# Fixing the place of the weight-scale sums and maxima in their engines' queues

## The chip, the cores and the metric

The kernel runs on one NeuronCore of a Trainium2 chip. The metric is the device time of one execution in microseconds; of the kernel before, three runs took 1717.04 to 1720.6 us, with a median of 1719.97 us.

## The reference

One layer of a streaming encoder is applied to 320 frames: 256 of a prompt and 64 of a sample, which share all weights. Cut to its weight products:

```python
xn = rmsnorm(x, norm_mix)
q, k, v, u, vs, g = split(xn @ w_in)           # 2048 -> 9216 columns
a  = stick_breaking_attention(q, k, v)         # prompt: causal; sample: with a cache of 256
bb = spatial_gate(gelu(u), rmsnorm(gelu(vs)))
merged = sigmoid(g_a) * (a @ w_branch_a) + sigmoid(g_b) * (bb @ w_branch_b)
h  = x + merged @ w_out
gu = rmsnorm(h, norm_ffn) @ w_gate_up          # 2048 -> 2 x 5632
h  = h + (silu(gu[..., :5632]) * gu[..., 5632:]) @ w_down
y  = rmsnorm(h, norm_final)
```

All of it is float32. The kernel has to return y, the new k and v rows and the sample's normalised v rows.

## The kernel before, in words

Features lie on the 128 partitions and the 320 frames along the free axis. Every weight matrix is read once, in **weight tiles** of 128 x 1024 float32 (512 KB, eight blocks of 128 x 128). A tile is loaded by a transfer that SP issues, split into a high part wh (ACT) and a low part wl (DVE), and used by PE in 24 products of 128 x 128 by 128 x 320: for each block wh with the activation's high part, wh with its low part, wl with its high part (lines 90, 91 and 92, in `product`). wh and wl have four buffers each, so ACT and DVE can be four tiles ahead of PE. The program counts tiles: `tick()` is called after the products of each, and `at(tick, fn)` runs a piece of code at that count.

The change concerns the **FFN**. Its 44 column groups are taken in three slices of 16, 16 and 12. A slice has a gate/up stage, then a down stage with w_down (float32 parts, wraw's three buffers; 32 tiles in slices one and two). A group is four tiles: two for the gate column block and two for the up column block. Below, tile (g,i) is tile i of group g.

Groups 0 to 2 run as float32 parts (`weights`, lines 82 and 83). From group 3 (`PLAIN`) on the products are in float16 (`block16`): wh is the weight times a power of two, rounded to float16 (ACT, line 785), wl the remainder (DVE, line 786), and the activations X are float16 pairs, made from h in `normed` (lines 747 on DVE, 749 on ACT, 750 on DVE). The power of two has to be known before the first wh of the group. It comes from a **scale** per group (`class Scale`):

- each raw tile gives one number per partition: the sum of magnitudes on ACT (`sum`, line 174) or the largest magnitude on DVE (`top`, line 170). From group 5 on tiles 0 and 2 get sums and tiles 1 and 3 maxima; groups 3 and 4 have four sums.
- `pack` (lines 180 and 182, DVE: topmost, packed) makes one number per partition of the four; `spread` (line 186, PE: one small product) lays it across all partitions; `close` (lines 190 to 192 and 777, DVE: peak, down, up, undo) makes the factors of it.

Raw tiles of these groups have a pool of their own, raw16, with 14 buffers. A load into it (line 759, issued by SP) must wait until the tile that had the buffer was read by its sum or maximum, its wh and its wl. The program text asks for these steps at fixed counts before the group's first product: the load of tile i at 11 − i tiles before it, the sum or maximum at 8 − i, the spread at 4, the closing at 3:

```python
at(max(start_of(j) - 11 + i, base + 1), group_load, j, i)
at(start_of(j) - 8 + i, group_top, j, i)
at(start_of(j) - 4, lambda j=j: groups[j]["scale"].spread())
at(start_of(j) - 3, group_close, j)
```

That is the order in which instructions are *traced*, not the order in which they stand in the queues. Each engine executes its queue strictly in order, and a scheduler fills the queues: it may put an instruction whose inputs it takes to be ready ahead of others that were traced before it. `tc.keep_in_program_order(ins)` takes this freedom away for one instruction: it stays behind the instruction that was traced last before it on its engine. Before the change the spread is fixed in this manner, sums and maxima are not. After the two blocks of a group, ACT takes the results out of PSUM (`finish16`, lines 821 and 822, ev with Silu and bb), DVE multiplies them (line 823) and the product is split into two parts A (line 128 on ACT, line 129 on DVE) for w_down.

Of the kernel before, what the change touches and what calls it, by code (L numbers as in the profile page):

```python
# [13 lines left out]
AF = mybir.ActivationFunctionType  # L14
ALU = mybir.AluOpType
# [25 lines left out]
def stream_step(ctx: ExitStack, tc: tile.TileContext, xT, w_in, w_a, w_b, w_out, w_gu, w_down,  # L41
                gains, ws_t, bs, ck_t, cv, y_t, k_t, v_t, sv_t):
    nc = tc.nc
# [119 lines left out]
    class Scale:  # L163
# [3 lines left out]
            self.tops = const.tile([P, n], F32, tag=f"tops{n}", bufs=2, name="tops")  # L167

        def top(self, i, src):
            nc.vector.tensor_reduce(out=self.tops[:, i : i + 1], in_=src, axis=mybir.AxisListType.X, op=ALU.max,  # L170
                                    apply_absolute_value=True)

        def sum(self, i, src, junk):
            nc.scalar.activation(out=junk, in_=src, func=AF.Abs, accum_out=self.tops[:, i : i + 1])  # L174

        def pack(self):
            own = self.tops
# [10 lines left out]
        def close(self):  # L188
            top, self.down, self.up = (const.tile([P, 1], F32, tag=t, bufs=3, name=t) for t in ("peak", "down", "up"))
            nc.vector.tensor_reduce(out=top, in_=self.row[:, :P], axis=mybir.AxisListType.X, op=ALU.max)  # L190
            nc.vector.tensor_tensor(out=self.down.bitcast(I32), in0=top.bitcast(I32), in1=bits, op=ALU.bitwise_and)
            nc.vector.tensor_tensor(out=self.up.bitcast(I32), in0=self.down.bitcast(I32), in1=bits, op=ALU.bitwise_xor)
            return self
# [782 lines left out]
```

## Time and profile before

| | before |
|---|---|
| median of three runs | 1719.97 us (1717.04 to 1720.6) |
| the profiled execution | 1719.68 us |
| its span, first to last instruction | 1717.9 us |
| PE busy | 1665.5 us, 97% |
| DVE busy | 979.6 us, 57% |
| ACT busy | 793.3 us, 46% |
| mean granted clock of PE | 0.996 |

The profile is one execution. Its page gives busy times, the span in 40 slices, DMA queues, the chain of work that ended last, and groups of instructions by line; further views give waits, a timeline and busy times by stretch. A row of the timeline is: start in us from the span's start, length in us, engine, line, operation, result and operands with their sizes, and how often; in brackets the idle time of the engine before it and what ended it. Raw buffers are called raw there whichever pool they are from. PE's products overlap in their pipeline: one is shown 0.30 us long, but the next starts 0.136 us later in the f16 stages.

### The profile page before, as it was taken

The numbers are of one execution on the slowest core, as the hardware profiler recorded it, in microseconds if no ns is written. First come the engines' busy times: TensorE is split into PE (matmuls) and PEld (weight loads), VectorE is DVE, ScalarE is ACT, GpSimd is POOL, SyncE is SP. The second block draws the span as 40 slices with busy tenths as digits, with TensorE's granted clock in tenths as the row PEclk, the third lists the DMA queues.
The fourth block names the chain that finished last, engine by engine and source line by source line (L and its number), as shares of the span: only waits on it lengthen the run. The fifth ranks groups of instructions, "written<-read, shape, count | busy, mean of one in ns | idle before, by whom it ended". The sixth has DMA issues, their size and how long they took to land.

```text
span 1717.9 us, 28001 instructions
## 1 busy us (share of the span) xinstructions
PE 1665.5 (97%) x11586; PEld 1493.7 (87%) x11586; DVE 979.6 (57%) x1430; ACT 793.3 (46%) x1117; POOL 56.9 (3%) x80
## 2 busy tenths in 40 slices
PE   9999999999999999999989899999988999999997
PEld 9999999999999999999656689976666899766797
DVE  6777656544444445559555554456556544556454
ACT  6655545433333334447545532354554423555442
POOL 1200021000000001110000000000000000000000
PEclk9999999999999999999999999999999999999999
DMA  7676656544444445567444455444444554443153
GB/s 256 182 218 169 172 169 169 155 149 147 150 152 152 149 155 169 174 207 256 144 135 143 140 171 149 147 145 138 139 144 136 170 149 141 144 139 99 55 149 122
DMA packets 100512, 268.33 MB, mean 156 GB/s; under 512 B 28993, under 2 KB 35393, under 8 KB 100385
## 3 DMA queue, kind: packets, MB, share of 16 engines
q1 hardware_dynamic: 97936, 261.36, 48.6%
q0 software_dynamic: 1312, 3.80, 0.7%
q8 instruction: 90, 1.47, 0.3%
q10 hardware_dynamic: 1136, 1.39, 0.2%
q14 instruction: 38, 0.30, 0.1%
HBM read 256.03 MB, written 5.51 MB: 152 GB/s over the span
## 4 chain that ended last, share of the span: by engine, by line
PE 68%; DMA 15%; ACT 7%; DVE 6%; issue 3%; ACTq 0%; DVEq 0%
PE acc L92 21%; PE acc L91 21%; PE acc L90 21%; DMA raw<-w_gu 15%; DVE wl L786 5%; ACT wh L785 4%; ACT junk L174 2%; PE aux L289 1%; ACT A L128 1%; PE acc L289 1%; DMA raw<-w_in 1%; PE aux L535 1%; DVE h L900 0%; DVE wl L83 0%; ACT wh L82 0%
## 5 line engine op out<-in xcount | busy, mean ns | idle before, releaser
L90 PE MATMUL acc<-A,wh 128*128 128x320 f32 x1856 | 574.9, 310 | 2.1 <-ACT wh L82 1.7
L92 PE MATMUL acc<-A,wl 128*128 128x320 f32 x1856 | 573.7, 309 | 1.4 <-DVE wl L83 1.4
L91 PE MATMUL acc<-A,wh 128*128 128x320 f32 x1856 | 573.7, 309 | 0.2
L82 ACT CAST wh<-raw 128x1024 fp32r<-128x1024 f32 (+1 forms) x304 | 311.5, 1026 | 521.6 <-PE acc L91 430.2
L83 DVE TENSOR_TENSOR wl<-raw,wh 128x1024 fp32r<-128x1024 f32 (+1 forms) x304 | 363.9, 1198 | 265.2 <-ACT wh L82 264.6
L92 PE MATMUL acc<-X,wl 128*128 128x320 f16 x1312 | 394.4, 301 | 32.8 <-DVE wl L786 32.7
L90 PE MATMUL acc<-X,wh 128*128 128x320 f16 x1312 | 393.9, 300 | 4.0 <-ACT wh L785 3.9
L91 PE MATMUL acc<-X,wh 128*128 128x320 f16 x1312 | 393.7, 300 | 0.0
L90 PEld LDWEIGHTS acc<-A,wh 128*128 128x128 f32 x1856 | 348.5, 188 | 3.3 <-ACT wh L82 2.3
L92 PEld LDWEIGHTS acc<-A,wl 128*128 128x128 f32 x1856 | 348.4, 188 | 1.9 <-DVE wl L83 1.9
L91 PEld LDWEIGHTS acc<-A,wh 128*128 128x128 f32 x1856 | 348.5, 188 | 0.7 <-DVE A L129 0.7
L786 DVE SCALAR_TENSOR_TENSOR wl<-raw,up,wh 128x1024 f16<-128x1024 f32 x164 | 209.8, 1280 | 176.3 <-ACT wh L785 173.8
L92 PEld LDWEIGHTS <-wl 128*128 128x128 f16 x1312 | 128.6, 98 | 99.4 <-DVE wl L786 49.3
L174 ACT ACTIVATE junk<-raw 128x1024 f16<-128x1024 f32 x86 | 90.9, 1056 | 264.5 <-DMA raw<-w_gu 264.4
L785 ACT ACTIVATE wh<-raw,up 128x1024 f16<-128x1024 f32 x164 | 180.3, 1137 | 29.9 <-PE acc L91 29.7
L90 PEld LDWEIGHTS <-wh 128*128 128x128 f16 x1312 | 128.8, 98 | 54.5 <-ACT wh L785 6.7
L91 PEld LDWEIGHTS <-wh 128*128 128x128 f16 x1312 | 128.8, 98 | 48.9
L170 DVE TENSOR_REDUCE tops<-raw 128x1 f32<-128x1024 f32 x78 | 94.6, 1213 | 3.1 <-DMA raw<-w_gu 3.0
L90 PE MATMUL acc<-mh,wh 128*128 128x320 f32 x256 | 79.2, 309 | 0.0
L90 PE MATMUL acc<-B,wh 128*128 128x320 f32 x256 | 79.1, 309 | 0.0
L91 PE MATMUL acc<-B,wh 128*128 128x320 f32 x256 | 79.1, 309 | 0.0
L92 PE MATMUL acc<-B,wl 128*128 128x320 f32 x256 | 79.1, 309 | 0.0
(206 smaller groups left out, 1299.4 us busy)
## 6 DMA issues: line engine op xcount, KB each, us to landing
raw<-w_gu SPq DMA_DIRECT2D x176, 512.0 KB, 3.7
raw<-w_in SPq DMA_DIRECT2D x141, 512.0 KB, 3.8
raw<-w_down SPq DMA_DIRECT2D x80, 512.0 KB, 3.6
raw<-w_out SPq DMA_DIRECT2D x32, 512.0 KB, 3.7
raw<-w_a SPq DMA_DIRECT2D x16, 512.0 KB, 3.6
raw<-w_b SPq DMA_DIRECT2D x16, 512.0 KB, 3.5
raw<-w_down SPq DMA_DIRECT2D x16, 256.0 KB, 2.7
x<-xT SPq DMA_DIRECT2D x8, 320.0 KB, 7.9
```

Source lines behind the costliest of these rows:

```text
L82: nc.scalar.copy(out=wh[:, : n * P], in_=raw[:, : n * P])
L83: nc.vector.tensor_tensor(out=wl[:, : n * P], in0=raw[:, : n * P], in1=wh[:, : n * P].bitcast(F32), op=ALU.subtract)
L90: nc.tensor.matmul(ps[:, :T], a, x[0], start=first, stop=False, skip_group_check=True)
L91: nc.tensor.matmul(ps[:, :T], a, x[1], start=False, stop=False, skip_group_check=True)
L92: nc.tensor.matmul(ps[:, :T], b, x[0], start=False, stop=last, skip_group_check=True)
L128: nc.scalar.copy(out=hi, in_=src)
L170: nc.vector.tensor_reduce(out=self.tops[:, i : i + 1], in_=src, axis=mybir.AxisListType.X, op=ALU.max, apply_absolute_value=True)
L174: nc.scalar.activation(out=junk, in_=src, func=AF.Abs, accum_out=self.tops[:, i : i + 1])
L289: nc.tensor.matmul(first[b][h][:, :T], w[:, (h * n + j) * P : (h * n + j + 1) * P], xs[c + j][i], start=not last and c + j + i == 0, stop= ...
L535: mm = lambda out, a, b, first, last: nc.tensor.matmul(out, a, b, start=first, stop=last, skip_group_check=True)
L785: nc.scalar.activation(out=wh, in_=raw, func=AF.Copy, scale=up)
L786: nc.vector.scalar_tensor_tensor(out=wl, in0=raw, scalar=up, in1=wh, op0=ALU.mult, op1=ALU.subtract)
```

## The change

Both operations on raw tiles are handed to `keep_in_program_order`, so that each stays behind what was traced just before it on DVE or on ACT. Nothing else is edited. Lines after the first edit move by one: what was line 174 is 175, line 785 is 786, and so on.

```diff
         def top(self, i, src):
-            nc.vector.tensor_reduce(out=self.tops[:, i : i + 1], in_=src, axis=mybir.AxisListType.X, op=ALU.max,
-                                    apply_absolute_value=True)
+            tc.keep_in_program_order(nc.vector.tensor_reduce(
+                out=self.tops[:, i : i + 1], in_=src, axis=mybir.AxisListType.X, op=ALU.max, apply_absolute_value=True))
 
         def sum(self, i, src, junk):
-            nc.scalar.activation(out=junk, in_=src, func=AF.Abs, accum_out=self.tops[:, i : i + 1])
+            tc.keep_in_program_order(
+                nc.scalar.activation(out=junk, in_=src, func=AF.Abs, accum_out=self.tops[:, i : i + 1]))
```

The queues of PE, POOL and SP hold the same instructions in the same order as before; those of ACT and DVE differ in the FFN alone, but for the maximum over the norm's gains, which moves on DVE from the start of the program to the w_out stage. Three places follow. In the names, a number marks a tile: (5,0) to (5,3) are raw_8362, raw_8406, raw_8445 and raw_8482, (6,0) is raw_8532, (7,0) to (7,3) are raw_8684, raw_8716, raw_8752 and raw_8787, (8,0) to (8,3) are raw_8836, raw_8868, raw_8904 and raw_8939, (9,0) is raw_8988.

The first is ACT in the middle of the first f16 stage, where the weights of group 5 are made. Before:

```order
L174 ACTIVATE junk,tops<-raw_8836 128x1024
L785 ACTIVATE wh_8799<-raw_8362,up 128x1024
L785 ACTIVATE wh_8838<-raw_8406,up 128x1024
L821 ACTIVATE ev<-acc,undo 128x320
L174 ACTIVATE junk,tops<-raw_8904 128x1024
L785 ACTIVATE wh_8871<-raw_8445,up 128x1024
L785 ACTIVATE wh_8906<-raw_8482,up 128x1024
L822 ACTIVATE bb<-acc,undo 128x320
L174 ACTIVATE junk,tops<-raw_8988 128x1024
```

and with the change:

```order
L175 ACTIVATE junk,tops<-raw_8684 128x1024
L128 CAST A<-bb 128x320
L786 ACTIVATE wh_8799<-raw_8362,up 128x1024
L786 ACTIVATE wh_8838<-raw_8406,up 128x1024
L822 ACTIVATE ev<-acc,undo 128x320
L175 ACTIVATE junk,tops<-raw_8752 128x1024
L786 ACTIVATE wh_8871<-raw_8445,up 128x1024
L786 ACTIVATE wh_8906<-raw_8482,up 128x1024
L823 ACTIVATE bb<-acc,undo 128x320
L175 ACTIVATE junk,tops<-raw_8836 128x1024
```

Beside the same wh there now stand the sums of tiles four loads older: (7,0), (7,2) and (8,0) in place of (8,0), (8,2) and (9,0).

The second is DVE at the same place. Before:

```order
L786 SCALAR_TENSOR_TENSOR wl_8800<-raw_8362,up,wh_8799 128x1024
L170 TENSOR_REDUCE tops<-raw_8868 128x1
L786 SCALAR_TENSOR_TENSOR wl_8839<-raw_8406,up,wh_8838 128x1024
L786 SCALAR_TENSOR_TENSOR wl_8872<-raw_8445,up,wh_8871 128x1024
L170 TENSOR_REDUCE tops<-raw_8939 128x1
L190 TENSOR_REDUCE peak<-aux 128x1
L180 TENSOR_REDUCE topmost<-tops 128x1
L191 TENSOR_TENSOR down<-peak,bits 128x1
L182 TENSOR_SCALAR packed<-topmost 128x1
```

and with the change:

```order
L787 SCALAR_TENSOR_TENSOR wl_8800<-raw_8362,up,wh_8799 128x1024
L787 SCALAR_TENSOR_TENSOR wl_8839<-raw_8406,up,wh_8838 128x1024
L787 SCALAR_TENSOR_TENSOR wl_8872<-raw_8445,up,wh_8871 128x1024
L170 TENSOR_REDUCE tops<-raw_8787 128x1
L191 TENSOR_REDUCE peak<-aux 128x1
L192 TENSOR_TENSOR down<-peak,bits 128x1
L193 TENSOR_TENSOR up<-down,bits 128x1
L778 TENSOR_SCALAR undo<-down,undo_7066 128x1
L170 TENSOR_REDUCE tops<-raw_8716 128x1
L824 TENSOR_TENSOR bb<-bb,ev 128x320
L181 TENSOR_REDUCE topmost<-tops 128x1
```

The maxima are those of group 7 in place of group 8, and that of (7,1) stands behind peak to undo, the closing of group 6: it was traced right after it. Behind topmost follow wl of (5,3), A's low half, packed of group 7 and then wl of (6,0).

The third is ACT at the start of the FFN, from the copies of the norm's factor on; the sums there are those of groups 3 and 4 (raw_7979, raw_8016, raw_8059 and raw_8104 are (3,0) to (3,3)). Before:

```order
L174 ACTIVATE junk,tops<-raw_7979 128x1024
L174 ACTIVATE junk,tops<-raw_8016 128x1024
L82 CAST wh<-raw 128x1024
L220 COPY root<-root 32x10 x3
L174 ACTIVATE junk,tops<-raw_8059 128x1024
L174 ACTIVATE junk,tops<-raw_8104 128x1024
L749 ACTIVATE X<-ev,gain_7064 128x320 x2
L174 ACTIVATE junk,tops<-raw_8159 128x1024
L749 ACTIVATE X<-ev,gain_7064 128x320 x2
```

and with the change:

```order
L221 COPY root<-root 32x10 x3
L750 ACTIVATE X<-ev,gain_7064 128x320 x4
L175 ACTIVATE junk,tops<-raw_7979 128x1024
L82 CAST wh<-raw 128x1024
L814 ACT_TABLE_LOAD
L814 ACTIVATE ev<-ev 128x320
L750 ACTIVATE X<-ev,gain_7064 128x320
L82 CAST wh<-raw 128x1024
L750 ACTIVATE X<-ev,gain_7064 128x320
L175 ACTIVATE junk,tops<-raw_8016 128x1024
L750 ACTIVATE X<-ev,gain_7064 128x320
L82 CAST wh<-raw 128x1024
```

The four sums of group 3 stood around the copies of root; now the first comes behind the first four X, and one follows in each round of X, sum, X and wh. Between two such rounds PE needs one plain tile. In the down stages the sums of the next slice's first groups, which stood at the end of the f16 stage before, now come between the last eight tiles of w_down.

## The prediction

> **What bounds the kernel now.** I read the page's engine and group tables first, then the table of waits, then the timeline of PE, ACT and DVE inside the stretches where PE is not full. PE is busy for 97% of the span, so a gain can only come from its holes. The group table says where they lie: a group's last two numbers are the engine's idle time ahead of it and what ended it.
>
> ```profile
> PE 1665.5 (97%) x11586; PEld 1493.7 (87%) x11586; DVE 979.6 (57%) x1430; ACT 793.3 (46%) x1117; POOL 56.9 (3%) x80
> ...
> L92 PE MATMUL acc<-X,wl 128*128 128x320 f16 x1312 | 394.4, 301 | 32.8 <-DVE wl L786 32.7
> ...
> L174 ACT ACTIVATE junk<-raw 128x1024 f16<-128x1024 f32 x86 | 90.9, 1056 | 264.5 <-DMA raw<-w_gu 264.4
> ...
> raw<-w_gu SPq DMA_DIRECT2D x176, 512.0 KB, 3.7
> ```
>
> PE's holes sit in the f16 gate/up products and end with wl from DVE. ACT, 46% busy, stands 264 us ahead of the sums (L174) waiting for a load. The table of waits adds who holds the loads back:
>
> ```profile
> ACT junk L174 <- DMA raw<-w_gu: 264.4, 77, 5.2
> ...
> SPq L759 <- DVE wl L786: 492.7, 149, 6.1
> ```
>
> A load into raw16 waits until wl has read the tile 14 loads earlier. The timeline of DVE, ACT and PE (start, length, what) shows these two waits closing into a ring:
>
> ```profile
> 873.08 1.28 DVE L786 SCALAR_TENSOR_TENSOR wl<-raw,up,wh 128x1024 f16<-128x1024 f32 x1 [0.56 <-ACT wh L785]
> ...
> 880.29 1.29 DVE L786 SCALAR_TENSOR_TENSOR wl<-raw,up,wh 128x1024 f16<-128x1024 f32 x1 [2.95 <-ACT wh L785]
> 881.50 1.22 DVE L170 TENSOR_REDUCE tops<-raw 128x1 f32<-128x1024 f32 x1
> 882.63 0.28 DVE L190 TENSOR_REDUCE peak<-aux 128x1 f32<-128x128 f32 x1
> ...
> 883.21 0.21 DVE L777 TENSOR_SCALAR undo<-down,undo 128x1 f32<-128x1 f32 x1
> ...
> 884.53 0.49 DVE L823 TENSOR_TENSOR bb<-bb,ev 128x320 f32<-128x320 f32 x1
> ```
>
> ```profile
> 878.07 1.06 ACT L174 ACTIVATE junk<-raw 128x1024 f16<-128x1024 f32 x1 [3.58 <-DMA raw<-w_gu]
> ...
> 879.13 2.17 ACT L785 ACTIVATE wh<-raw,up 128x1024 f16<-128x1024 f32 x2
> 881.21 0.51 ACT L822 ACTIVATE bb<-acc,undo 128x320 f32<-128x320 f32 x1
> ...
> 885.16 1.06 ACT L174 ACTIVATE junk<-raw 128x1024 f16<-128x1024 f32 x1 [3.44 <-DMA raw<-w_gu]
> ...
> 886.21 0.44 ACT L128 CAST A<-bb 128x320 fp32r<-128x320 f32 x1
> ```
>
> ```profile
> 874.42 0.31 PE L92 MATMUL acc<-X,wl 128*128 128x320 f16 x1 [0.88 <-DVE wl L786]
> 881.64 0.31 PE L92 MATMUL acc<-X,wl 128*128 128x320 f16 x1 [0.52 <-DVE wl L786]
> 889.08 0.31 PE L92 MATMUL acc<-X,wl 128*128 128x320 f16 x1 [0.69 <-DVE wl L786]
> ```
>
> The wl that starts at 873.08 ends at 874.36; 3.71 us later, the landing time of a load, the sum at 878.07 starts; wh stands right behind that sum in ACT's queue, wl at 880.29 waits for wh, and its end at 881.57 releases the next load, whose sum starts at 885.16. Once around is 3.7 + 1.06 + 1.1 + 1.28 = 7.1 us, plus 0.44 where the cast to A lies between, and it feeds two weight tiles. PE's stalls come 7.22 and 7.44 us apart. **Latency in a ring, not any engine's work, sets the pace there.**
>
> What two tiles cost without the ring is in the trace too, at the start of the second and third f16 stage, where no stall occurs:
>
> ```profile
> 803.21 0.23 PE L186 MATMUL aux<-turner,packed 128*128 128x128 bf16 x1
> ...
> 994.51 0.30 PE L92 MATMUL acc<-X,wl 128*128 128x320 f16 x1
> ...
> 1110.15 0.23 PE L186 MATMUL aux<-turner,packed 128*128 128x128 bf16 x1
> ...
> 1341.25 0.30 PE L92 MATMUL acc<-X,wl 128*128 128x320 f16 x1
> ...
> 1457.27 0.23 PE L186 MATMUL aux<-turner,packed 128*128 128x128 bf16 x1
> ...
> 1470.38 0.22 PE L186 MATMUL aux<-turner,packed 128*128 128x128 bf16 x1
> ...
> 1621.67 0.30 PE L92 MATMUL acc<-X,wl 128*128 128x320 f16 x1
> ```
>
> From spread to spread, 1457.27 to 1470.38, a group of four tiles takes 13.11 us, so a tile 3.27.
>
> **What can be taken back.** The f16 stages hold 13, 16 and 12 groups. First stage: 803.21 to 994.65 (the last product plus one pitch of 0.14) is 191.4 us, against 13 × 13.11 = 170.4: 21.0 lost. Second: 231.2 against 209.8: 21.4. Third: 164.5 against 157.3: 7.2. Together **49.6 us**. The two down stages between them lose a little as well. There one tile takes 3.52 us, the step from one wh to the next, which wait for PE:
>
> ```profile
> 1043.19 1.05 ACT L82 CAST wh<-raw 128x1024 fp32r<-128x1024 f32 x1 [2.47 <-PE acc L91]
> ...
> 1046.71 1.05 ACT L82 CAST wh<-raw 128x1024 fp32r<-128x1024 f32 x1 [2.47 <-PE acc L91]
> ```
>
> 32 tiles are 112.6 us; from 994.65 to 1110.15 it took 115.5 and from 1341.39 to 1457.27 it took 115.9, so 2.9 + 3.3 = **6.2 us**, lost at their heads, where wh and wl come late out of the same ring. All of it: 55.8 us.
>
> **The change, part by part.** No instruction is added or removed on any engine, and the queues of PE, SP and POOL are the same. ACT's 86 sums and DVE's 78 maxima stand one group, four tiles, later. Take PE working on group 4 from time 0: it is through its tiles at 3.3, 6.5, 9.8 and 13.1, and starts group 5 at 13.1. With the durations above (L821 like L822, L129 like L823, each small step 0.2 like undo) and ACT in the new order:
>
> - wh of (5,0) can start when PE frees the buffer of (4,0), at 3.3, and ends 4.4; (5,1) 6.5 to 7.7; gate's eviction L821 to 8.2; sum (7,2) to 9.4; wh (5,2) 9.8 to 10.9; (5,3) 13.1 to 14.2; L822 to 14.8; sum (8,0) to 16.0; cast to A to 16.4; wh (6,0) to 17.6.
> - DVE: wl (5,2) to 12.2; max (7,3) to 13.4; peak, down, up, undo, which need the spread that PE runs at 13.1, to 14.2; max (7,1) to 15.4; L823 to 15.9; topmost to 16.1; wl (5,3) to 17.3; A's low half to 17.8; packed (7) to 18.0; wl (6,0) to 19.3; then (6,1) at 22.1 and (6,2) at 25.3, which is 12.2 + 13.1: the round closes in PE's own time.
>
> PE needs wl (6,0) at 26.5, it is there 7 us sooner; the tightest of the four, (5,3), has 5.8. packed (7) is asked for at 26.2: 8 us in hand. The sum's load is no longer in the round: tile (7,2) goes into the buffer of (4,0), whose wl ended 13.1 us before that of (5,0), thus at 19.3 − 26.2 = −6.9; plus 3.7 it lands at −3.2 and is summed at 8.2, **11 us of slack** where ACT now waits 3.5. So the stalls of the steady part go entirely, and I credit 49.6 + 6.2.
>
> What moves the other way is the start of the FFN. Before, eight sums slip in ahead; now the four of group 3 come between the plain tiles, and packed (3) may come after PE asks for it:
>
> ```profile
> 760.84 0.31 PE L90 MATMUL acc<-A,wh 128*128 128x320 f32 x1
> ...
> 768.59 1.98 POOL L215 TENSOR_TENSOR root<-ms,mhalf 32x10 f32<-32x10 f32 x1 [11.70 <-DVE ms L213]
> ...
> 770.96 0.62 ACT L220 COPY root<-root 32x10 f32<-32x10 f32 x3
> ...
> 775.87 1.02 ACT L749 ACTIVATE X<-ev,gain 128x320 f16<-128x320 f32 x2
> ...
> 778.89 1.28 ACT L813 ACT_TABLE_LOAD   x1
> ```
>
> PE asks after eight tiles, at 760.84 + 8 × 3.52 = 789.0. ACT's copies of root cannot come sooner than POOL's 770.57. Three sums between them and the fourth X go, but X also waits for ev from DVE, so I let that X end only 0.5 before the 776.9 of now, at 776.4. Then to the last sum of group 3: four sums (4.2), four wh (4.2), the table load (1.3), a Silu (0.5, like L822) and six X (3.1), 13.3 in all: 789.7, and topmost and packed 0.7 later, 790.4. **A single stall of 1.4 us**; bounds are 0, should X end 1.4 us sooner still, and 4, should each later X wait half a microsecond for ev. Behind it group 3's tiles run with one to two us in hand, then the round above is reached. At the later stages the same step has room: the sums of the next groups come from the 25th down tile on, PE asks at the 28th, and ACT is four tiles ahead.
>
> [...] While the ring runs, the clock falls twice (window, engine busy times, then granted clock):
>
> ```profile
> 890.00:900.00 10.00, 8.05 (x52) 4.99 (x50) 4.72 (x11) 3.64 (x5) 0.00 (x0) 0.90 0.42 129
> 900.00:910.00 10.00, 10.00 (x71) 7.01 (x70) 5.57 (x6) 4.67 (x7) 0.00 (x0) 0.93 0.50 159
> 1110.00:1170.00 60.00, 60.00 (x447) 43.26 (x446) 35.98 (x56) 31.69 (x44) 0.00 (x0) 1.00 0.42 141
> 1320.00:1330.00 10.00, 9.65 (x59) 6.46 (x60) 7.78 (x14) 4.42 (x8) 0.00 (x0) 0.83 0.40 133
> ```
>
> Clocks of 0.90, 0.93 and 0.83 over 10 us each are 1.0, 0.7 and 1.7 us of PE. I count these 3.4 us among the stalls, since the full 60 us carry 1.00. [...]
>
> **The sum.** The profiled execution took 1719.68 us, 0.3 below the median of the three runs. 1719.7 − 55.8 + 1.4 = **1665.3 us**.
>
> **Rivals.**
> *Half stays* (chance 0.10). The order closes a new, shorter ring, by DVE's peak: it waits for PE's spread, and a max, wl (5,3) and wl (6,0) are queued behind it. For: DVE now stands there at PE's pace. Against: it is reached at 13.4, after the spread, and 5.8 us remain. If every second stall comes back: 1665.3 + 28 = 1693 us.
> *No change* (0.03). The load itself, not its place in ACT's queue, is the limit, and wh waits where the sum did. For: SP waits 492.7 us for wl. Against: the first product of a tile lies 14 tiles, 45 us, behind the wl that frees its buffer. 1720 us.
> *Slower* (0.05). The sums are too late for the scale: PE reaches the spread before packed and stops, with all products behind it. That costs 41 times the lateness and decides once packed is more than 8 + 1.4 us later than in my round (55.8 / 41 = 1.4 to break even). For: the first group, where I find it late already. Against: 8 us in every other group. Stops of 3 us at each spread would give 1665.3 + 41 × 3 = 1789 us.
>
> **How the numbers follow.** All stalls gone: 0.82, its own range 1660 to 1673 (a first stall of 0 to 4 us, 3.4 for the clock, a few us where the stages meet, 0.2% between runs). That is already 8 in 10 of all cases; I reach up to 1680 for a part of the first rival. 0.2%, 3.4 us, is about what a measurement of this kernel tells from no change: faster 0.92, same 0.03, slower 0.05.
>
> **What would show it.** Right: ACT's idle time ahead of the sums for a load falls from 264 us to under 20; PE's for wl (L92, X) from 32.7 to under 3; spreads 13.1 us apart all through the stages; one stall near 789. Wrong: spreads 13.5 or more apart, or the clock dips with no stall near them. What would make it wrong at one stroke is a load that lands much later than 3.7 us.

## The result, and the profile after

The change makes the kernel faster: **1662.97 us** (median, 1662.5 to 1663.12) against 1719.16 us for the kernel before, run beside it on the same chip (1717.04 to 1720.6). The ratio is 0.9674, with a 95% interval of 0.9657 to 0.969. The forecast was 1665.3, in a range of 1659 to 1680. The profiled execution took 1663.03 us, with a span of 1660.9.

The page of the kernel after, in the order of the page before: the engines, the chain of work that ended last (its shares by engine), the groups, the loads. Line numbers from 174 on are one higher than before.

```profile
PE 1649.9 (99%) x11586; PEld 1498.3 (90%) x11586; DVE 979.8 (59%) x1430; ACT 804.3 (48%) x1117; POOL 56.6 (3%) x80
...
PE 97%; DMA 1%; DVE 1%; ACT 0%; SPq 0%; issue 0%; DVEq 0%; ACTq 0%
...
L92 PE MATMUL acc<-X,wl 128*128 128x320 f16 x1312 | 392.7, 299 | 0.0
...
L786 ACT ACTIVATE wh<-raw,up 128x1024 f16<-128x1024 f32 x164 | 188.1, 1148 | 217.4 <-PE acc L91 213.7
...
L175 ACT ACTIVATE junk<-raw 128x1024 f16<-128x1024 f32 x86 | 89.9, 1045 | 0.0
...
raw<-w_gu SPq DMA_DIRECT2D x176, 512.0 KB, 4.1
```

PE's idle time for wl is gone (32.7 us before, 0.0 now), and so is ACT's 264 us ahead of the sums. ACT now stands 213.7 us ahead of wh, and what ends that wait is PE freeing a buffer. Before, ACT was late for PE; now PE is late for ACT, as it should be when PE is the bound. The chain of work that ended last is PE's to 97% now; in the profile before, its shares were:

```profile
PE 68%; DMA 15%; ACT 7%; DVE 6%; issue 3%; ACTq 0%; DVEq 0%
```

A load takes slightly longer to land (4.1 us where it was 3.7), and no sum or maximum waits for it.

ACT in the middle of the first f16 stage, from the timeline of the kernel after:

```profile
881.21 1.15 ACT L786 ACTIVATE wh<-raw,up 128x1024 f16<-128x1024 f32 x1 [2.11 <-PE acc L91]
...
882.67 1.04 ACT L175 ACTIVATE junk<-raw 128x1024 f16<-128x1024 f32 x1
...
887.78 1.15 ACT L786 ACTIVATE wh<-raw,up 128x1024 f16<-128x1024 f32 x1 [2.11 <-PE acc L91]
...
889.25 1.04 ACT L175 ACTIVATE junk<-raw 128x1024 f16<-128x1024 f32 x1
```

No sum has a wait in brackets; the two wh shown wait 2.1 us for PE, and those between them 0.25 and 0.66. Two tiles take 6.57 us (881.21 to 887.78), where the ring took 7.22 and 7.44.

PE's timeline gives the account by stage, since the same products stand at its borders as before:

```profile
759.88 0.31 PE L90 MATMUL acc<-A,wh 128*128 128x320 f32 x1
...
788.35 0.23 PE L187 MATMUL aux<-turner,packed 128*128 128x128 bf16 x1 [0.15 <-DVE packed L183]
...
802.56 0.23 PE L187 MATMUL aux<-turner,packed 128*128 128x128 bf16 x1
...
907.33 0.22 PE L187 MATMUL aux<-turner,packed 128*128 128x128 bf16 x1
920.43 0.22 PE L187 MATMUL aux<-turner,packed 128*128 128x128 bf16 x1
...
972.62 0.30 PE L92 MATMUL acc<-X,wl 128*128 128x320 f16 x1
...
1085.53 0.23 PE L187 MATMUL aux<-turner,packed 128*128 128x128 bf16 x1
...
1294.88 0.30 PE L92 MATMUL acc<-X,wl 128*128 128x320 f16 x1
...
1407.79 0.23 PE L187 MATMUL aux<-turner,packed 128*128 128x128 bf16 x1
...
1564.75 0.30 PE L92 MATMUL acc<-X,wl 128*128 128x320 f16 x1
```

With 0.14 us added to each last product, as in the prediction:

| stretch | before, us | after, us | gain | predicted |
|---|---|---|---|---|
| up to the FFN's first product | 760.8 | 759.9 | 1.0 | 0 |
| plain tiles to the first border | 42.4 | 42.7 | -0.3 | -1.4 |
| f16 stage 1 | 191.4 | 170.2 | 21.2 | 21.0 |
| f16 stage 2 | 231.2 | 209.5 | 21.7 | 21.4 |
| f16 stage 3 | 164.5 | 157.1 | 7.4 | 7.2 |
| two down stages | 231.4 | 225.5 | 5.8 | 6.2 |
| from the last f16 product to the span's end | 96.1 | 96.0 | 0.1 | 0 |

These add up to 56.9 us, and the spans differ by 57.0. The 1.0 us at the program's start is not credited to the change: it lies in front of the FFN, and that start came between 759.46 and 761.32 in the experiments below.

### The profile page after: what moved, and what is told of

Same layout as the page of the kernel before. It is cut to its first block, busy times and chain, and to the rows that moved or that the text cites. A ratio compares the mean times of both kernels' runs of the same rounds, so it can differ in the third digit from the quotient of the medians.

```text
span 1660.9 us, 27999 instructions
## 1 busy us (share of the span) xinstructions
PE 1649.9 (99%) x11586; PEld 1498.3 (90%) x11586; DVE 979.8 (59%) x1430; ACT 804.3 (48%) x1117; POOL 56.6 (3%) x80
## 4 chain that ended last, share of the span: by engine, by line
PE 97%; DMA 1%; DVE 1%; ACT 0%; SPq 0%; issue 0%; DVEq 0%; ACTq 0%
PE acc L91 31%; PE acc L90 31%; PE acc L92 31%; PE aux L290 1%; PE acc L290 1%; DMA raw<-w_gu 1%; PE aux L536 1%; DMA raw<-w_in 1%; DVE h L901 0%; DVE wl L83 0%; PE aux L652 0%; PE aux L466 0%; DVE X L751 0%; PE aux L187 0%; PE aux L469 0%
## 5 line engine op out<-in xcount | busy, mean ns | idle before, releaser
L92 PE MATMUL acc<-A,wl 128*128 128x320 f32 x1856 | 574.2, 309 | 0.0
L92 PE MATMUL acc<-X,wl 128*128 128x320 f16 x1312 | 392.7, 299 | 0.0
L92 PEld LDWEIGHTS acc<-A,wl 128*128 128x128 f32 x1856 | 348.5, 188 | 0.0
L786 ACT ACTIVATE wh<-raw,up 128x1024 f16<-128x1024 f32 x164 | 188.1, 1148 | 217.4 <-PE acc L91 213.7
L92 PEld LDWEIGHTS <-wl 128*128 128x128 f16 x1312 | 128.4, 98 | 49.9
L92 PE MATMUL acc<-mh,wl 128*128 128x320 f32 x256 | 79.2, 309 | 0.0
L91 PE MATMUL acc<-ml,wh 128*128 128x320 f32 x256 | 79.2, 309 | 0.0
L90 PE MATMUL acc<-B,wh 128*128 128x320 f32 x256 | 79.2, 309 | 0.0
```

The costliest lines, as they stand in the source:

```text
L90: nc.tensor.matmul(ps[:, :T], a, x[0], start=first, stop=False, skip_group_check=True)
L91: nc.tensor.matmul(ps[:, :T], a, x[1], start=False, stop=False, skip_group_check=True)
L92: nc.tensor.matmul(ps[:, :T], b, x[0], start=False, stop=last, skip_group_check=True)
L786: nc.scalar.activation(out=wh, in_=raw, func=AF.Copy, scale=up)
```

## The experiments

Two theories stood at the start. **The ring**, as in the prediction: ACT's sum waits for a load, the wh behind it in ACT's queue is late with it, wl is late, and wl's end is what lets the next load start. The rival: **the slack**: what counts is only how far the raw tile's readers run ahead of PE, or that the order is fixed at all, so that less slack is always worse and the engine that holds the waiting instruction does not matter.

**Which engine's order matters.** The change has two edits, so each was run alone. In the first, only the sums on ACT are fixed and the maxima are left to the scheduler:

```diff
-            tc.keep_in_program_order(nc.vector.tensor_reduce(
-                out=self.tops[:, i : i + 1], in_=src, axis=mybir.AxisListType.X, op=ALU.max, apply_absolute_value=True))
+            nc.vector.tensor_reduce(out=self.tops[:, i : i + 1], in_=src, axis=mybir.AxisListType.X, op=ALU.max,
+                                    apply_absolute_value=True)
```

> Only ACT's sums are fixed; DVE's maxima stand where the scheduler puts them, beside wl of the group three before. Theory (a ring: load, operation on the raw tile, wh or wl, next load): the ring through ACT is open. A second one, through DVE, is left: load 3.7 + max 1.2 + wl 1.3 = 6.2 us for one pair of tiles and, with the closing of 0.8 in between, 7.0 for the other, together 13.2 against PE's 13.1, so 0.1 to 0.5 us a group stays: 1667 to 1685 us. ACT's wait for loads ahead of the sums under 20 us. Rival 'the maxima were the cause': 1710 us or more. Rival 'either edit is enough': 1663 us.

Measured: 1663.41 us, ratio 0.9662 (0.9648 to 0.9677). The sums alone bring the whole gain; the 1667 to 1685 us that were expected were missed. There is indeed a chain of this kind through DVE. First two rows of the table of waits, then DVE's timeline in the first and in the second f16 stage:

```profile
ACT A L128 <- DVE bb L824: 80.3, 41, 6.2
...
DVE tops L170 <- DMA raw<-w_gu: 60.7, 64, 3.3
```

```profile
818.86 1.22 DVE L170 TENSOR_REDUCE tops<-raw 128x1 f32<-128x1024 f32 x1 [2.27 <-DMA raw<-w_gu]
...
923.57 1.22 DVE L170 TENSOR_REDUCE tops<-raw 128x1 f32<-128x1024 f32 x1 [2.39 <-DMA raw<-w_gu]
...
1124.96 1.22 DVE L170 TENSOR_REDUCE tops<-raw 128x1 f32<-128x1024 f32 x1 [1.23 <-DMA raw<-w_gu]
...
1228.77 1.22 DVE L170 TENSOR_REDUCE tops<-raw 128x1 f32<-128x1024 f32 x1 [0.26 <-DMA raw<-w_gu]
```

DVE's maxima wait 60.7 us for loads, as ACT's sums did before. The wait also reaches ACT: its cast to A, with wh queued behind it, stands 80.3 us for the bb that comes after the maximum on DVE. Yet PE waits nowhere but for the 0.15 us at the start of the FFN. Eight turns of the chain, of four tiles each, lie between 818.86 and 923.57: 13.09 us a turn, PE's own pace, with single turns from 12.8 to 13.3. Between 1124.96 and 1228.77 eight turns take 12.98 us each. The expectation had worked the turn as 13.2 us, 0.1 longer than PE's 13.1; the trace has it no longer than PE's, so the delay doesn't grow. A wait for a load is no loss by itself; it is one when the turn of the ring is longer than PE's. The margin here is about 0.1 us a turn, and how much more this chain would bear was not tried.

The second run fixes the maxima and leaves the sums to the scheduler:

```diff
-            tc.keep_in_program_order(
-                nc.scalar.activation(out=junk, in_=src, func=AF.Abs, accum_out=self.tops[:, i : i + 1]))
+            nc.scalar.activation(out=junk, in_=src, func=AF.Abs, accum_out=self.tops[:, i : i + 1])
```

> Only DVE's maxima are fixed; ACT's sums stand where the scheduler puts them, twelve tiles ahead of the wh behind them. Theory: the ring through ACT stays, 3.7 + 1.06 + 1.1 + 1.3 = 7.1 to 7.3 us for two tiles against 6.55 without it: 1705 to 1720 us, and ACT waits 200 us or more for loads ahead of the sums. Rival 'the maxima were the cause': 1663 to 1680 us.

Measured: 1707.27 us, ratio 0.992 (0.9904 to 0.9937). The time is in the expected range; the size of ACT's wait is not. From its table of waits:

```profile
ACT junk L174 <- DMA raw<-w_gu: 133.8, 42, 4.9
...
PE acc L92 <- DVE wl L786: 32.6, 35, 1.2
```

Half of ACT's wait for loads is gone, and PE still waits as long for wl as before (32.7). By stage, in the profiled execution (1703.28 us, the fastest of four), the f16 stages take 185.1, 226.7 and 166.3 us, 41 more than after the change, and the down stages 112.8 each. Its span is 16.4 us shorter than that of the kernel before (1701.5 for 1717.9): 9.1 of it lie in the f16 stages, 5.9 at the heads of the down stages and 1.4 in front of the FFN. The ring through ACT is still there: every other sum waits now (42 waits for 77), and where it turns PE has one stall of 1.2 us a group in place of two shorter ones, in about half of these groups with a short one beside it. So it is the sums' place on ACT that makes the difference.

**Fixed order, but early.** If the place counts and not the fixing, sums that are fixed four tiles further ahead must bring the loss back:

```diff
-            at(max(start_of(j) - 11 + i, base + 1), group_load, j, i)
-            at(start_of(j) - 8 + i, group_top, j, i)
+            at(max(start_of(j) - 15 + i, base + 1), group_load, j, i)
+            at(max(start_of(j) - 12 + i, base + 2), group_top, j, i)
```

> Sums and maxima fixed as in the change, but traced twelve tiles ahead of their group's first product and not eight (loads traced fifteen ahead), so that beside a wh stands the sum of the same tile as before the change. Theory: only the distance matters; the ring closes again in fixed order, 14.5 us a group: 1712 to 1725 us. Rival 'what helped is that the order is fixed, not where': 1663 to 1668 us.

Measured: 1712.55 us, ratio 0.9951 (0.9936 to 0.9966), as expected. From its table of waits:

```profile
ACT junk L175 <- DMA raw<-w_gu: 209.4, 60, 5.4
...
PE acc L92 <- DVE wl L787: 22.1, 28, 1.2
...
PE acc L92 <- DVE packed L183: 11.7, 10, 1.2
```

209.4 us of waiting for loads are back, and with them the stalls. The row with packed belongs to them: these products (L92) read wl, and packed stands right behind a wl on DVE and ends less than 0.1 us after it (for the product that starts at 903.74, the wl ends at 903.68 and packed at 903.74). Not all of the 49.6 us over the change are the ring's: the plain part takes 49.1 us here instead of 42.7, because eight sums crowd into the start of the FFN and wh of a plain tile comes late once by 4.2 us (at 785.01; the row is in the last section). The f16 stages lose 42 us.

Between 8 and 12 lies 11, with the loads left where they are:

```diff
-            at(start_of(j) - 8 + i, group_top, j, i)
+            at(max(start_of(j) - 11 + i, base + 2), group_top, j, i)
```

> Fourteen buffers, sums and maxima fixed eleven tiles ahead (three sooner than the change, one later than the run with twelve). Ring theory: three tiles a turn of 7.3 us against PE's 9.8: 1663 to 1670 us. Rival 'the time follows the distance gradually': 1695 us or more. At the start of the FFN sums come sooner than in the change, which can give back the 0.2 us stall there.

Measured: 1662.71 us, ratio 0.9665 (0.9651 to 0.968); ACT waits for loads 5.5 us in all. One tile nearer than 12, and nothing is lost. (The run with twelve also moved the loads' place in the program, so this step is of two edits; that from ten to eleven buffers below is of one.)

**The other end of the same distance.** The sum of a tile must wait for the wl that frees its buffer, so taking buffers away must act like summing earlier. raw16 got fewer:

```diff
-        raw = late.tile([P, HALF * P], F32, tag="raw16", bufs=14, name="raw16")
+        raw = late.tile([P, HALF * P], F32, tag="raw16", bufs=10, name="raw16")
```

> The changed kernel with its order, but ten raw16 buffers and not fourteen. Theory: a sum's tile then gets the buffer of a tile whose wl is two tiles before the wh behind the sum, which is the relation of the kernel before; slack 11 - 13 = -2 us, the ring closes: 1710 to 1725 us. Rival 'the order in the queues itself made the gain': 1663 to 1668 us. Rival 'loads are limited by their number in flight': slower than 1725 us.

> The changed kernel with eleven buffers, same place of the sums. Ring theory: a sum's tile gets the buffer of a tile three before the wh behind the sum; that load starts with the wl of an odd tile, and a chain of 7.3 us comes three tiles (9.8 us) further: full speed, 1663 to 1668 us; ACT begins to wait for loads, under 150 us in all. Slack theory: 11 - 10 = +1 us, the same, with ACT waiting hardly at all. Rival 'a gain that grows with the number of buffers': about 1695 us, between ten and fourteen.

> The changed kernel with twelve buffers. Ring theory and slack theory both: four tiles a turn, slack 11 - 6.5 = 4.7 us, 1663 to 1666 us, no wait of ACT for loads ahead of the sums over 20 us. Rival 'number of buffers': about 1680 us.

Measured: 1716.65 us with ten (ratio 0.9975, 0.996 to 0.999), 1662.56 with eleven (0.9666, 0.9652 to 0.9681), 1662.68 with twelve (0.9665, 0.9649 to 0.9681). The first is as expected. The other two run at full speed as expected, 0.4 and 0.3 us under their ranges; so did the run with 11 ahead, 0.3 under. Ten buffers, waits first, then ACT's and DVE's timelines:

```profile
ACT junk L175 <- DMA raw<-w_gu: 238.6, 66, 5.8
```

```profile
899.11 1.06 ACT L175 ACTIVATE junk<-raw 128x1024 f16<-128x1024 f32 x1 [3.45 <-DMA raw<-w_gu]
...
906.85 1.06 ACT L175 ACTIVATE junk<-raw 128x1024 f16<-128x1024 f32 x1 [3.74 <-DMA raw<-w_gu]
907.90 2.17 ACT L786 ACTIVATE wh<-raw,up 128x1024 f16<-128x1024 f32 x2
...
914.14 1.06 ACT L175 ACTIVATE junk<-raw 128x1024 f16<-128x1024 f32 x1 [3.65 <-DMA raw<-w_gu]
```

```profile
909.07 1.28 DVE L787 SCALAR_TENSOR_TENSOR wl<-raw,up,wh 128x1024 f16<-128x1024 f32 x1 [4.90 <-ACT wh L786]
```

This is the picture of the kernel before, with the order of the kernel after: the sum waits for its load, wh follows it at once, wl follows wh and ends at 910.35; 3.79 us later the next sum starts. The turns are 7.74 and 7.29 us. The same program with 11 buffers runs at PE's pace, with 13.4 us of waits for loads on ACT in all, the longest 2.8.

These points follow from one number of the prediction, the 11 us by which a sum's load is early. A tile is 3.28 us of PE's time. Summing 11 ahead, or three buffers fewer, takes 9.8 us of it and leaves 1.2; 12 buffers leave 4.4; one more tile in either direction leaves -2.1. Measured waits of ACT for loads: 0 with 12 buffers, 5.5 and 13.4 us at a slack of 1.2, 209.4 and 238.6 at -2.1. There is no gentle slope: once the load lands after the sum's turn, the loss feeds itself by the ring, and **2 us too little cost 42 us of the f16 stages in the one run and 53 in the other**.

**Nine buffers, where both theories missed.** With nine, worked by the ring alone, the chain from a load to the next release would come out shorter than PE's pace; by slack it would be worse than with ten:

```diff
-        raw = late.tile([P, HALF * P], F32, tag="raw16", bufs=14, name="raw16")
+        raw = late.tile([P, HALF * P], F32, tag="raw16", bufs=9, name="raw16")
```

> The changed kernel with nine raw16 buffers. The scheduler, with the same rule, then puts ACT's two sums of a group one or two places further back: (g+2,0) between wh (g,1) and (g,2), (g+2,2) between wh (g,2) and (g,3). Ring theory: from wl (g,1) the chain is load 3.7, sum 1.06, wh 1.15, eviction and cast 1.0, two wh 2.3, wl 1.3 = 10.4 us and has come four tiles further; from wl (g,3) it is 3.7 + two sums and two wh 4.4 + 1.3 = 9.4 for four. Both are under the 13.1 us that PE needs for four tiles: nothing is held back, 1663 to 1672 us, faster than with ten buffers. Rival 'slack by number of buffers' (11 us of slack less 3.27 for each buffer fewer: 11 - 16 = -5): slower than with ten, 1720 us or more.

Measured: 1698.99 us, ratio 0.9872 (0.985 to 0.9894). Less slack than with ten is faster by 17.7 us, so slack does not set the size of the loss; but the ring does not vanish either. DVE's and ACT's timelines, and the page's row on the loads with their median landing time:

```profile
901.37 2.47 DVE L787 SCALAR_TENSOR_TENSOR wl<-raw,up,wh 128x1024 f16<-128x1024 f32 x2
...
914.41 1.27 DVE L787 SCALAR_TENSOR_TENSOR wl<-raw,up,wh 128x1024 f16<-128x1024 f32 x1
...
915.67 2.47 DVE L787 SCALAR_TENSOR_TENSOR wl<-raw,up,wh 128x1024 f16<-128x1024 f32 x2
```

```profile
909.77 1.06 ACT L175 ACTIVATE junk<-raw 128x1024 f16<-128x1024 f32 x1 [2.31 <-DMA raw<-w_gu]
...
910.83 1.13 ACT L786 ACTIVATE wh<-raw,up 128x1024 f16<-128x1024 f32 x1
...
913.30 2.18 ACT L786 ACTIVATE wh<-raw,up 128x1024 f16<-128x1024 f32 x2
```

```profile
raw<-w_gu SPq DMA_DIRECT2D x176, 512.0 KB, 4.6
```

One turn takes 14.30 us for four tiles: wl of (g,1) ends at 903.84 and wl of (g+1,1) at 918.14. With ten buffers the turn above took 15.03 (899.11 to 914.14), and PE needs 13.1. The same rows show, by the places given in the expectation, where the chain of 10.4 us was too short:

- The load released at 903.84 is summed at 909.77, 5.9 us later and not 3.7. Its wl is the last of three that run one behind the other, as those from 914.41 to 918.14 do, so three loads are released within 2.5 us; the median landing is 4.6 us, for 3.7 in the kernel before.
- Eviction and cast take 1.3 us (911.96 to 913.30), where 1.0 was reckoned.
- wl of (g+1,1) ends 2.7 us after its wh (915.48), not 1.3: wl of (g,3) still has to go first, and it starts at 914.41 though its wh was done at 911.96, because bb, a maximum and two other steps stand before it on DVE.

Together 2.2 + 0.3 + 1.4 us, which with 10.4 make the 14.3. They are read from one turn; no run changed one of them alone. With nine buffers the scheduler also places the sums one or two places further back, so this is not a change of one size alone.

## Why the prediction was right

- **What bounds the kernel.** Right. The turn of the ring is set by latencies, and it came back each time ACT's sum was put ahead of its load's landing: by sums fixed 12 tiles ahead, and by ten buffers under the new order.
- **What can be taken back.** Right to 0.3 us in each f16 stage (21.2, 21.7 and 7.4 for 21.0, 21.4 and 7.2) and to 0.4 in the down stages (5.8 for 6.2). A group without the ring was said to take 13.11 us; the spreads at 907.33 and 920.43 are 13.10 apart.
- **The new order's timetable.** Right. Counted from the start of PE's group at 881.13 (the spread at 894.24 less 13.11), the first sum was put at 8.2 and the second at 14.8 us; those at 889.25 and 882.67, the latter one round of 13.11 earlier, stand at 8.1 and 14.7. DVE's packed was put at 18.0. From DVE's and PE's timelines of the kernel after, which belong to the same round:

```profile
885.36 0.15 DVE L183 TENSOR_SCALAR packed<-topmost 128x1 bf16<-128x1 f32 x1
...
894.24 0.22 PE L187 MATMUL aux<-turner,packed 128*128 128x128 bf16 x1
```

  packed of the group ends at 885.51, which is 17.5 of the round that began 13.1 earlier, and PE uses it at 894.24: 8.7 us in hand, where 8 were worked out. The 11 us of slack of the load hold as well; the runs at 11 and 12 bracket where it is used up, to one tile.
- **The start of the FFN.** The right place and cause, but mis-sized: a stall of 0.15 us at 788.35, and 0.3 us in the whole stretch, for the 1.4 of the sum. The larger part is the time of the fourth X. ACT and DVE of the kernel after:

```profile
773.49 1.02 ACT L750 ACTIVATE X<-ev,gain 128x320 f16<-128x320 f32 x2 [1.03 <-DVE ev L748]
...
786.21 1.04 ACT L175 ACTIVATE junk<-raw 128x1024 f16<-128x1024 f32 x1
...
788.15 0.15 DVE L183 TENSOR_SCALAR packed<-topmost 128x1 bf16<-128x1 f32 x1
```

  The X ends at 774.51, 14.6 us after the FFN's first product; the prediction had 776.4 after a first product at 760.84, so 15.6. The wait for ev that was thought to keep it there is 1.0 us long. From there to the last sum of group 3 took 12.7 us for 13.3, and topmost and packed another 1.05 for 0.7. The lower bound of 0 was nearly met.
- **The clock.** The 3.4 us were rightly counted with the stalls. Between 760 and 1620 us no window of 10 us of the kernel after has a granted clock below 1.00. Two of the three stretches of time that were low before:

```profile
890.00:900.00 10.00, 10.00 (x77) 7.20 (x74) 7.76 (x14) 5.74 (x9) 0.00 (x0) 1.00 0.42 142
900.00:910.00 10.00, 10.00 (x77) 7.23 (x75) 5.98 (x12) 6.35 (x9) 0.00 (x0) 1.00 0.59 193
```

  The last section shows the holes that had a dip behind them.
- **Rivals.** "Half stays" named peak on DVE as a new ring: peak waits for the spread three times, 0.9 us each, once at the end of each f16 stage, and no product is late for it. "No change" had the load itself as the limit: loads land no sooner now (4.1 us), and no sum waits for one. SP's long wait for wl, the argument for it, is still there (421.9 us in 147 waits, where it was 492.7) and costs nothing. "Slower" asked for packed to come over 9.4 us later than worked out; it is there 8.7 us before its use in the group shown, and 0.15 late once. A truly late scale was not tried. (In these sums 14 tiles are 46 us, not 45, and 41 stops of 3 us give 1788 us, not 1789.)
- **The remaining 2.3 us** between 1665.3 and 1663.0 are 1.1 of the first stall, 1.0 of the program's start, not credited to the change, and 0.4 of the stages and the tail, less 0.3 by which more time lies outside the span now (2.1 us for 1.8).

Nothing that was tried beats the change: it, sums alone, 11 ahead, and 11 or 12 buffers all lie between 1662.6 and 1663.4 us, at PE's pace.

## What to carry to other kernels

Where an engine with much idle time waits for a load at the head of its queue, follow that wait around: if what is queued behind it ends in the instruction that frees the buffer for the next load, latencies and not work set the pace, and the cost of one turn against the bounding engine's time for the same tiles tells whether there is a loss. That holds as far as the turn is known: the chain through DVE, worked as 0.1 us too long, cost nothing, and the one with nine buffers, worked as short enough, did cost. Such a ring is left by putting more tiles between the release of a buffer and the use of its next load: here by consuming the load later (11 tiles ahead for 12) or with one buffer more (11 for 10). More buffers in the old order, or a faster step on ACT or DVE, were not tried. The slack can be worked out in tiles; it says where the loss begins, not how large it is. A row with a large wait for a load is no proof of a loss (60.7 us on DVE cost nothing), since only a ring that turns slower than the bound costs time.

## What was not expected of the hardware

**The granted clock dips behind some holes and not behind others of their size.** In the kernel before, PE's timeline shows that the first dip begins right after two stalls close together:

```profile
896.58 0.31 PE L90 MATMUL acc<-X,wh 128*128 128x320 f16 x1 [1.08 <-ACT wh L785]
...
897.90 0.44 PE L92 MATMUL acc<-X,wl 128*128 128x320 f16 x1 [0.87 <-DVE wl L786]
898.13 0.47 PE L90 MATMUL acc<-X,wh 128*128 128x320 f16 x1
898.40 0.47 PE L91 MATMUL acc<-X,wh 128*128 128x320 f16 x1
...
901.33 0.32 PE L90 MATMUL acc<-X,wh 128*128 128x320 f16 x1
```

From 897.9 to 901.3 the products start 0.27 us apart instead of 0.136: half the rate, for 3.4 us. The second dip, at 1321, follows the same pair, 1.06 and 0.87 us. The sums fixed 12 ahead have a dip behind the 4.2 us stall, and nine buffers have one behind a single stall of 2.02 us. The granted clock is 0.83 from 780 to 790 in the first, and 0.91 and 0.92 from 1200 to 1220 in the second. PE's timelines of the two:

```profile
785.01 0.42 PE L90 MATMUL acc<-A,wh 128*128 128x320 f32 x1 [4.21 <-ACT wh L82]
...
786.71 0.47 PE L90 MATMUL acc<-A,wh 128*128 128x320 f32 x1
```

```profile
1207.27 0.31 PE L92 MATMUL acc<-X,wl 128*128 128x320 f16 x1 [2.02 <-DVE packed L183]
```

Stalls of that size do not always cost clock: with nine buffers others of 2.44 and 2.47 us (at 857.40 and 1294.61) are followed by windows at 1.00, and the maxima alone or ten buffers have some 20 stalls of 1.2 us each and not one dip. What is shown is that the dips went where the holes went; what decides which hole has one behind it is not: no run moved a hole by itself.
